# Top-k of the expert lookup: maxima beside the projections, lookups in bf16 between weight blocks

## The chip, the cores and the metric

One NeuronCore of a Trainium2 chip runs the whole program in one launch. The metric is device time in microseconds (us). The kernel before took 1478.95 us, the median of three runs (1477.77 to 1479.18).

## What is computed

The reference is a network of two blocks over 256 positions of width 1024, in float32. Only one part of it concerns the change: a layer of 16384 small experts (128 x 128 of them, reached by pairs of keys), with 8 heads.

```python
def peer_ffn(h, w_q, sub_keys, u, v):
    qh = (h @ w_q).reshape(t, PEER_HEADS, 2, PEER_HALF)
    s = jnp.einsum('thcd,hcnd->thcn', qh, sub_keys)
    s1, i1 = lax.top_k(s[:, :, 0], PEER_TOPK)          # 16 of 128, for each head
    s2, i2 = lax.top_k(s[:, :, 1], PEER_TOPK)
    cand = (s1[..., :, None] + s2[..., None, :])        # 256 sums
    cand_idx = (i1[..., :, None] * N_KEYS + i2[..., None, :])
    top_s, pos = lax.top_k(cand, PEER_TOPK)             # 16 of 256
    eidx = jnp.take_along_axis(cand_idx, pos, axis=-1)
    g = jax.nn.softmax(top_s, axis=-1)
    pre = jnp.einsum('cd,chkd->chk', hc, u[ec])
    coef = gc * jax.nn.gelu(pre, approximate=False)
    return jnp.einsum('chk,chkd->cd', coef, v[ec])
```

The kernel does not gather: it multiplies all experts' `u` with all positions, weighs the products by a routing matrix that holds the gates (zero where an expert was not chosen), and multiplies with all of `v`.

## The kernel before, in words

Weights come in blocks of 128 x 1024 float32 (512 KB). `weights` (L92) loads a block on SyncE's queue into one of four `wraw` buffers, rounds it on ScalarE to a high half `wh` (L98) and subtracts on an engine of choice to the low half `wl` (L100): "v" is VectorE, "g" is GpSimd. There are three buffers of `wh` and `wl`. A product block (`fm_block`, L133) is 24 products on TensorE, three for each of eight slices: high by high (L129), high by low (L130), low by high (L131), so the third product of a block is the first to need `wl`.

`peer` (L752) has these stages.

- The layer's input `hn` is made by `adaln` on VectorE and ScalarE (L278 to L281). 16 blocks of `peer_wq` give the queries `q`, one key set `j` each (head and half); the first two blocks are interleaved slice by slice. Low halves: blocks 0 and 1 on GpSimd, the others on VectorE. The sub-keys `sk` (1 MB) are loaded once (L767).
- `topk(tb)` for two blocks of 128 positions: the scores (L800, four key sets in one bank, copied by L801), then on VectorE the sixteen largest of each of 16 lists of 128 with their places (L803 to L807: eight largest, their places, replace, again), the 256 sums of each head (L810), sixteen of each of 8 lists of 256 (L815 to L819), and the lookup of the two key numbers by comparison, product and sum over 16 (L821 to L831), in float32.
- 128 blocks of `u` (`u_block`). The first 38, 43 and 46 (`N_PRE`) run while `topk` is going on, with their low halves on GpSimd; behind 38 come the exponentials (`exps`), behind 43 the gates (`gates`), transposed by TensorE (L849) into `rt`.
- 32 steps of `route`, eight positions each, make the routing matrix from five one-hot operations on VectorE (L882, L890) and 24 products (L895), and weigh what the u blocks left (L898); between them stand 2 and 3 u blocks in turn (`ROUTE_PER`), low halves on VectorE. Then the last u blocks, then 128 blocks of `v`.

The order on each engine is set at compile time by a planner, which takes the instructions by their place in the program among those that its own model holds ready, so that the instructions of two lists may be interleaved; on the chip each engine keeps that order. `issue_after` pins an instruction behind another of the same engine.

Of the kernel before, what the change touches and what calls it, by code (L numbers as in the profile page):

```python
# [9 lines left out]
FT = mybir.dt.float32  # L10
FR = mybir.dt.float32r
BF = mybir.dt.bfloat16
U32 = mybir.dt.uint32
AF = mybir.ActivationFunctionType
OP = mybir.AluOpType
# [9 lines left out]
TAKEN = -3.4e38  # L25
# [4 lines left out]
PLAN = "ijjaavaasvqvqvksskkssksqssrgrqsssrgss0gr1rggr0rrrgrg1rg20g31rg2rrg3rrgg23rg"  # L30
SPLIT = 4
FIRST = 2
N_PRE = (38, 43, 46)
ROUTE_PER = (2, 3)


class Scratch:
# [33 lines left out]
class Net:  # L71
# [104 lines left out]
    def sums(self, pool, cols=None):  # L176


        nc = self.nc
        n = 1 if cols is None else cols.shape[2]  # L180
        ps = self.ps([128, 2, n], "sm")
        behind = []

        def put():
            j, sq = behind.pop()
            rhs = self.ones[:, :1] if cols is None else cols[:, j]
            for tb in range(2):
                self.last_sum = nc.tensor.matmul(ps[:, tb], sq[:, tb * 128:tb * 128 + 128], rhs,  # L188
                                                 start=j == 0 and tb == 0, stop=j == KT - 1, skip_group_check=True)

        def take(x, j):
            if behind:
                put()
            sq = pool.tile([128, T], FT, name="sq", bufs=3)
            nc.scalar.activation(sq, x[:, j], AF.Square)
            behind.append((j, sq))

        def done():
            put()
            return ps  # L200
        return take, done
# [550 lines left out]
    def peer(self):  # L752
# [3 lines left out]
        with ExitStack() as es:  # L756
# [5 lines left out]
            def carve(name, *shape, dtype=FT):  # L762
                return tail.tile([128, *shape], dtype, name=name)
# [6 lines left out]
            for k in range(KT):  # L770
                o = slice(k * 128, k * 128 + 128)
                for ps, w in zip(pss, ws):
                    self.mm3(ps, (w[0][:, o], w[1][:, o]), (hn[0][:, k], hn[1][:, k]), k == 0, k == KT - 1)
            for j in range(16):
                ps = pss[j] if j < FIRST else self.fm_block(self.weights(ap["peer_wq"][j]), hn)
                nc.scalar.activation(q[:, j], ps, AF.Copy)
            io = self.io128
            rt = P.tile([128, 5, T], BF, name="rt")
            iob = P.tile([128, 128], BF, name="iob")
            nc.gpsimd.tensor_copy(iob, io)  # L780
            s_all = [carve(f"s{tb}", 16, 128) for tb in range(2)]
            cand = carve("cand", 8, 16, 16)
            prod = carve("prod", 128, 16)
            v16 = carve("v16", 16, 16)
            i16 = carve("i16", 16, 16, dtype=U32)
            i16f = carve("i16f", 8, 2, 16)
            top = carve("top", 8, 16)
            pos = carve("pos", 8, 16, dtype=U32)
            pc = carve("pc", 2, 128, dtype=U32)
            pf = i16.rearrange("p a b -> p (a b)").bitcast(FT).rearrange("p (c k) -> p c k", c=2)  # L790
            ies = [carve(f"ie{tb}", 3, 128) for tb in range(2)]

            def topk(tb):
                s = s_all[tb]
                ie = ies[tb]
                for g in range(4):
                    ps = self.ps([128, 4, 128], "acc")
                    for i in range(4):
                        j = 4 * g + i
                        nc.tensor.matmul(ps[:, i], q[:, j, tb * 128:tb * 128 + 128], sk[:, j], start=True, stop=True)  # L800
                    nc.scalar.activation(s[:, 4 * g:4 * g + 4], ps, AF.Copy)  # L801
                for j in range(16):
                    nc.vector.max(out=v16[:, j, :8], in_=s[:, j])  # L803
                    nc.vector.max_index(out=i16[:, j, :8], in_max=v16[:, j, :8], in_values=s[:, j])
                    nc.vector.match_replace(out=s[:, j], in_to_replace=v16[:, j, :8], in_values=s[:, j], imm_value=TAKEN)
                    nc.vector.max(out=v16[:, j, 8:], in_=s[:, j])
                    nc.vector.max_index(out=i16[:, j, 8:], in_max=v16[:, j, 8:], in_values=s[:, j])  # L807
                nc.vector.tensor_copy(i16f.rearrange("p h c k -> p (h c) k"), i16)
                v4 = v16.rearrange("p (h c) k -> p h c k", c=2)
                nc.vector.tensor_tensor(cand, v4[:, :, 0, :, None].to_broadcast([128, 8, 16, 16]),  # L810
                                        v4[:, :, 1, None, :].to_broadcast([128, 8, 16, 16]), op=OP.add)
                cf = cand.rearrange("p h a b -> p h (a b)")
                for h in range(8):
                    c = cf[:, h]
                    nc.vector.max(out=top[:, h, :8], in_=c)  # L815
                    nc.vector.max_index(out=pos[:, h, :8], in_max=top[:, h, :8], in_values=c)
                    nc.vector.match_replace(out=c, in_to_replace=top[:, h, :8], in_values=c, imm_value=TAKEN)
                    nc.vector.max(out=top[:, h, 8:], in_=c)
                    nc.vector.max_index(out=pos[:, h, 8:], in_max=top[:, h, 8:], in_values=c)  # L819
                posf = pos.rearrange("p h k -> p (h k)")  # L820
                nc.vector.tensor_scalar(pc[:, 0], posf, 4, None, op0=OP.logical_shift_right)  # L821
                nc.vector.tensor_scalar(pc[:, 1], posf, 15, None, op0=OP.bitwise_and)
                nc.vector.tensor_copy(pf, pc)
                eq = s.rearrange("p a (b c) -> p (a b) c", c=16)
                for c in range(2):
                    nc.vector.tensor_tensor(eq, io[:, None, :16].to_broadcast([128, 128, 16]),
                                            pf[:, c, :, None].to_broadcast([128, 128, 16]), op=OP.is_equal)
                    nc.vector.tensor_tensor(prod.rearrange("p (h k) j -> p h k j", h=8),
                                            eq.rearrange("p (h k) j -> p h k j", h=8),
                                            i16f[:, :, c, None, :].to_broadcast([128, 8, 16, 16]), op=OP.mult)  # L830
                    nc.vector.tensor_reduce(ie[:, c], prod, axis=AX.X, op=OP.add)  # L831
                g = ie[:, 2].rearrange("p (h k) -> p h k", h=8)
                nc.vector.tensor_tensor(g, top, top[:, :, 0:1].to_broadcast([128, 8, 16]), op=OP.subtract)

            def exps():
                with tc.issue_after(self.last_act.ins):
# [3 lines left out]
            def gates(tb):  # L840
                ie = ies[tb]
                g = ie[:, 2].rearrange("p (h k) -> p h k", h=8)
                st = P.tile([128, 8], FT, name="gst")
                nc.vector.tensor_reduce(st, g, axis=AX.X, op=OP.add)
                nc.vector.reciprocal(st, st)
                nc.vector.tensor_tensor(g, g, st[:, :, None].to_broadcast([128, 8, 16]), op=OP.mult)
                ps = self.ps([128, 3, 128], "sm")
                for c in range(3):
                    nc.tensor.transpose(ps[:, c], ie[:, c], self.ident)  # L849
                ts = slice(tb * 128, tb * 128 + 128)  # L850
                nc.vector.tensor_copy(rt[:, :2, ts], ps[:, :2])
                g = ps[:, 2]
                for z in range(3):
                    nc.vector.tensor_copy(rt[:, 2 + z, ts], g)
                    if z < 2:
                        nc.vector.tensor_tensor(ie[:, 0], g, rt[:, 2 + z, ts], op=OP.subtract)
                        g = ie[:, 0]

            def u_block(e, t, eng):

                ps = self.fm_block(self.weights(ap["peer_u"][e], eng), hn, out=self.ps([128, T], ("mm", "acc", "acc")[e % 3]))
                if t:
                    g = W.tile([128, T], FT, name="gelu", bufs=1)
                    self.last_act = nc.scalar.activation(g[:, :t], ps[:, :t], AF.Gelu)
                    nc.vector.tensor_mul(big[:, e, :t], big[:, e, :t], g[:, :t])
                if t < T:
                    self.last_act = nc.scalar.activation(big[:, e, t:], ps[:, t:], AF.Gelu)
# [30 lines left out]
                    nc.vector.tensor_mul(w[:, :n], pt[:, :n], w[:, :n])  # L898
                    nc.scalar.activation(w[:, n:], pt[:, n:], AF.Copy)

            topk(0)
            topk(1)
            e = 0
            for n, step in zip(N_PRE, (exps, lambda: [gates(tb) for tb in range(2)], lambda: 0)):
                while e < n:
                    u_block(e, 0, "g")
                    e += 1
                step()
            d = repeat(0)
# [608 lines left out]
```

## Time and profile before

| | |
|---|---|
| median of three runs | 1478.95 us |
| the profiled execution | 1477.79 us, span 1476.0 us |
| PE (TensorE) busy | 1389.3 us, 94% |
| DVE (VectorE) busy | 1103.3 us, 75% |
| ACT (ScalarE) busy | 755.4 us, 51% |
| POOL (GpSimd) busy | 247.5 us, 17% |
| mean granted TensorE clock | 0.982 |

Times in the rows are microseconds from the span's start, durations of a group's members nanoseconds. An arrow names what ended a wait. The busy time of PE overlaps itself, since products are pipelined: the number that a stretch started says more. The stage of this change lies from about 290 to 490 us: GpSimd has nearly all of its work between 355 and 482 us, DVE is full from 347 us on, PE is nearly full.

### The profile page before, as it was taken

The page shows a single profiled execution, that of the slowest core. Times are in us where ns is not written, and L with a number is a line of the kernel's source. Part 1 is how long each engine was busy: PE and PEld are TensorE (multiplying, and loading weights), DVE is VectorE, ACT ScalarE, POOL GpSimd, SP SyncE. Part 2 cuts the span into 40 slices and gives each one's busy share as a digit, 9 for nine tenths or more (in the row PEclk, how much of TensorE's full clock was granted, in tenths as well). Part 3 has the DMA queues.
Part 4 walks back from the last instruction along what each step waited for, and adds up shares of the span by engine and source line. Part 5 has one row for each costly group of instructions (what it writes and reads, how often), then busy time and mean ns, then how long its engine had stood idle before and what let it go on. Part 6 is the DMA issues. An engine that isn't in the chain of part 4 may idle for free. (4 is left out here: it accounts for less than half of the span.)

```text
span 1476.0 us, 28894 instructions
## 1 busy us (share of the span) xinstructions
PE 1389.3 (94%) x11584; PEld 1334.0 (90%) x11584; DVE 1103.3 (75%) x2044; ACT 755.4 (51%) x1358; POOL 247.5 (17%) x102
## 2 busy tenths in 40 slices
PE   4987988989998999999999999999999999899997
PEld 3876878989998999999999999999999889789996
DVE  7677868646999988999966555666557786777776
ACT  4544635445445555555454444444445465655555
POOL 3356532105999000000000000000000000000001
PEclk9999989999999999999999999999999999999998
DMA  7765854654555555555566665776564445256562
GB/s 281 250 199 201 280 175 161 205 193 156 174 184 166 173 154 168 158 159 157 165 194 216 202 190 190 228 233 215 186 187 157 128 134 171 72 173 196 189 191 95
DMA packets 76235, 269.52 MB, mean 183 GB/s; under 512 B 8970, under 2 KB 11202, under 8 KB 75460
## 3 DMA queue, kind: packets, MB, share of 16 engines
q1 hardware_dynamic: 71426, 257.99, 54.5%
q10 hardware_dynamic: 4674, 9.69, 1.9%
q8 instruction: 90, 1.47, 0.4%
q14 instruction: 45, 0.37, 0.1%
HBM read 265.01 MB, written 4.21 MB: 182 GB/s over the span
## 5 line engine op out<-in xcount | busy, mean ns | idle before, releaser
L98 ACT ACTIVATE wh<-wraw 128x1024 fp32r<-128x1024 f32 x431 | 456.2, 1060 | 521.1 <-PE ps_acc L130 243.1
L100 DVE TENSOR_TENSOR wl<-wraw,wh 128x1024 fp32r<-128x1024 f32 x346 | 423.9, 1227 | 245.3 <-ACT wh L98 243.9
L129 PE MATMUL ps_acc<-c,wh 128*128 128x256 f32 x1024 | 286.5, 280 | 0.0
L131 PE MATMUL ps_acc<-c,wl 128*128 128x256 f32 x1024 | 286.4, 280 | 0.0
L130 PE MATMUL ps_acc<-c,wh 128*128 128x256 f32 x1024 | 286.4, 280 | 0.0
L100 POOL TENSOR_TENSOR wl<-wraw,wh 128x1024 fp32r<-128x1024 f32 x85 | 228.1, 2700 | 194.0 <-ACT wh L98 151.2
L131 PE MATMUL ps_acc<-hn,wl 128*128 128x256 f32 x696 | 192.7, 277 | 6.2 <-POOL wl L100 6.2
L131 PE MATMUL ps_mm<-hn,wl 128*128 128x256 f32 x680 | 191.3, 282 | 6.4 <-POOL wl L100 6.4
L129 PE MATMUL ps_mm<-hn,wh 128*128 128x256 f32 x680 | 194.7, 286 | 2.0 <-ACT sga L446 1.0
L129 PE MATMUL ps_acc<-hn,wh 128*128 128x256 f32 x696 | 193.9, 279 | 0.0
L129 PEld LDWEIGHTS ps_acc<-c,wh 128*128 128x128 f32 x1024 | 192.5, 188 | 0.1
L130 PE MATMUL ps_acc<-hn,wh 128*128 128x256 f32 x696 | 192.4, 277 | 0.1
L130 PEld LDWEIGHTS ps_acc<-c,wh 128*128 128x128 f32 x1024 | 192.5, 188 | 0.0
L131 PEld LDWEIGHTS ps_acc<-c,wl 128*128 128x128 f32 x1024 | 192.5, 188 | 0.0
L130 PE MATMUL ps_mm<-hn,wh 128*128 128x256 f32 x680 | 191.5, 282 | 0.0
L1404 POOL TENSOR_TENSOR big<-big 128x512 f32<-128x512 f32 x4 | 5.0, 1264 | 982.0 <-DVE big L1401 982.0
L131 PEld LDWEIGHTS ps_mm<-hn,wl 128*128 128x128 f32 x680 | 130.8, 192 | 7.2 <-POOL wl L100 7.2
L131 PEld LDWEIGHTS ps_acc<-hn,wl 128*128 128x128 f32 x696 | 130.7, 188 | 7.2 <-POOL wl L100 7.2
L129 PEld LDWEIGHTS ps_mm<-hn,wh 128*128 128x128 f32 x680 | 131.3, 193 | 4.6 <-issue 1.3
L130 PEld LDWEIGHTS ps_mm<-hn,wh 128*128 128x128 f32 x680 | 131.0, 193 | 0.2
L130 PEld LDWEIGHTS ps_acc<-hn,wh 128*128 128x128 f32 x696 | 130.8, 188 | 0.3 <-DVE hn L281 0.3
L129 PEld LDWEIGHTS ps_acc<-hn,wh 128*128 128x128 f32 x696 | 130.6, 188 | 0.1
(484 smaller groups left out, 2821.9 us busy)
## 6 DMA issues: line engine op xcount, KB each, us to landing
wraw<-in_peer_u_dram SPq DMA_DIRECT2D x128, 512.0 KB, 3.9
wraw<-in_peer_v_dram SPq DMA_DIRECT2D x128, 512.0 KB, 4.2
wraw<-in_w_in_dram SPq DMA_DIRECT2D x70, 512.0 KB, 4.4
wraw<-in_ffn_up_dram SPq DMA_DIRECT2D x44, 512.0 KB, 3.6
wraw<-in_ffn_down_dram SPq DMA_DIRECT2D x22, 512.0 KB, 3.6
ada<-in_w_ada_dram SPq DMA_DIRECT2D x16, 512.0 KB, 6.5
wraw<-in_w_out_dram SPq DMA_DIRECT2D x16, 512.0 KB, 4.5
wraw<-in_peer_wq_dram SPq DMA_DIRECT2D x16, 512.0 KB, 3.6
```

The costliest lines, as they stand in the source:

```text
L98: nc.scalar.activation(h, raw, AF.Copy)
L100: (nc.vector if eng == "v" else nc.gpsimd).tensor_tensor(l, raw, h.bitcast(FT), op=OP.subtract)
L129: mm(out, a[0], b[0], start=first, stop=False, **kw)
L130: mm(out, a[0], b[1], start=False, stop=False, **kw)
L131: self.last_mm = mm(out, a[1], b[0], start=False, stop=last, **kw)
L1404: nc.gpsimd.tensor_tensor(xf[:, tb, cs], xt[:, tb, cs], fg[:, cs], op=OP.mult)
```

## The change

- The score products of a key set are issued in the loop over the key sets, behind the next set's projection, both blocks of positions in one bank; the scores are copied for each set, and its two lists' maxima follow there. The low halves of the `peer_wq` blocks in that loop go to GpSimd for three of four, to VectorE for the fourth (blocks 2, 4, 5, 6 to GpSimd, 3 and 7 to VectorE, and so on).
- Then come the sums of both blocks of positions, and the sixteen largest of all 16 lists of 256.
- The lookups compare, multiply and add in bf16 for both key numbers at once: 4096 elements an operation; the positions are first repeated four times by ScalarE (`pf4`). The sum over 16 is by halving adds. Each block of positions is done in four steps, one step ahead of each u block from block 18 to 25.
- GpSimd makes the low halves of the first 18 u blocks, VectorE those of all others. `exps` comes behind block 27, `gates` behind 29, the routing behind 31, with 3, 3, 3 and 2 u blocks between steps in turn, which leaves nine for the end instead of two.
- The candidates lie in `q`'s memory.

```diff
--- before.py
+++ after.py
@@ -30,8 +30,9 @@
 PLAN = "ijjaavaasvqvqvksskkssksqssrgrqsssrgss0gr1rggr0rrrgrg1rg20g31rg2rrg3rrgg23rg"
 SPLIT = 4
 FIRST = 2
-N_PRE = (38, 43, 46)
-ROUTE_PER = (2, 3)
+N_PRE = (27, 29, 31)
+ROUTE_PER = (3, 3, 3, 2)
+ONLY_MAXIMA = 18
 
 
 class Scratch:
@@ -771,66 +772,88 @@
                 o = slice(k * 128, k * 128 + 128)
                 for ps, w in zip(pss, ws):
                     self.mm3(ps, (w[0][:, o], w[1][:, o]), (hn[0][:, k], hn[1][:, k]), k == 0, k == KT - 1)
+            scores = carve("s", 32, 128).rearrange("p (t j) n -> p t j n", t=2)
+            v16 = carve("v16", 32, 16).rearrange("p (t j) k -> p t j k", t=2)
+            i16 = carve("i16", 32, 16, dtype=U32).rearrange("p (t j) k -> p t j k", t=2)
+
+            def sixteen(val, pos, of):
+
+                for half in (slice(0, 8), slice(8, 16)):
+                    nc.vector.max(out=val[:, half], in_=of)
+                    nc.vector.max_index(out=pos[:, half], in_max=val[:, half], in_values=of)
+                    if half.start == 0:
+                        nc.vector.match_replace(out=of, in_to_replace=val[:, half], in_values=of, imm_value=TAKEN)
+
+            def keys(j):
+
+                ps = self.ps([128, 2, 128], "sm")
+                for tb in range(2):
+                    nc.tensor.matmul(ps[:, tb], q[:, j, tb * 128:tb * 128 + 128], sk[:, j], start=True, stop=True)
+                nc.scalar.activation(scores[:, :, j], ps, AF.Copy)
+                for tb in range(2):
+                    sixteen(v16[:, tb, j], i16[:, tb, j], scores[:, tb, j])
+
             for j in range(16):
-                ps = pss[j] if j < FIRST else self.fm_block(self.weights(ap["peer_wq"][j]), hn)
+                ps = pss[j] if j < FIRST else self.fm_block(self.weights(ap["peer_wq"][j], "gggv"[j % 4]), hn)
                 nc.scalar.activation(q[:, j], ps, AF.Copy)
+                if j:
+                    keys(j - 1)
+            keys(15)
             io = self.io128
             rt = P.tile([128, 5, T], BF, name="rt")
             iob = P.tile([128, 128], BF, name="iob")
             nc.gpsimd.tensor_copy(iob, io)
-            s_all = [carve(f"s{tb}", 16, 128) for tb in range(2)]
...
+            cand = q.rearrange("p a (b c) -> p (a b c)", b=16).rearrange("p (t h x) -> p t h x", t=2, h=8)
+
+            def half(name, n):
+                return carve(name, n // 2).bitcast(BF)
+            i16f = half("i16f", 512).rearrange("p (t c h k) -> p t c h k", t=2, c=2, h=8)
+            top = carve("top", 2, 8, 16)
+            pos = carve("pos", 2, 8, 16, dtype=U32)
+            pc = carve("pc", 4, 128, dtype=U32).rearrange("p (t c) x -> p t c x", t=2)
+            pf = half("pf", 512).rearrange("p (t x) -> p t x", t=2)
+            pf4 = half("pf4", 1024).rearrange("p (x a) -> p x a", a=4)
             ies = [carve(f"ie{tb}", 3, 128) for tb in range(2)]
 
-            def topk(tb):
-                s = s_all[tb]
+            def sums():
+
+                for tb in range(2):
+                    v4 = v16[:, tb].rearrange("p (h c) k -> p h c k", c=2)
+                    nc.vector.tensor_tensor(cand[:, tb].rearrange("p h (a b) -> p h a b", a=16),
+                                            v4[:, :, 0, :, None].to_broadcast([128, 8, 16, 16]),
+                                            v4[:, :, 1, None, :].to_broadcast([128, 8, 16, 16]), op=OP.add)
+                    nc.vector.tensor_copy(i16f[:, tb].rearrange("p c h k -> p h c k"),
+                                          i16[:, tb].rearrange("p (h c) k -> p h c k", c=2))
+
+            def lookup(tb):
+
                 ie = ies[tb]
-                for g in range(4):
...
+                posf = pos[:, tb].rearrange("p h k -> p (h k)")
+                nc.vector.tensor_scalar(pc[:, tb, 0], posf, 4, None, op0=OP.logical_shift_right)
+                nc.vector.tensor_scalar(pc[:, tb, 1], posf, 15, None, op0=OP.bitwise_and)
+                nc.vector.tensor_copy(pf[:, tb], pc[:, tb].rearrange("p c x -> p (c x)"))
+                yield
+                nc.scalar.activation(pf4, pf[:, tb, :, None].to_broadcast([128, 256, 4]), AF.Copy)
+                eq, prod = (scores[:, i].rearrange("p a b -> p (a b)").bitcast(BF) for i in range(2))
+                shape = [128, 256, 4, 4]
+                nc.vector.tensor_tensor(eq.rearrange("p (x a b) -> p x a b", a=4, b=4),
+                                        iob[:, :16].rearrange("p (a b) -> p a b", a=4)[:, None].to_broadcast(shape),
+                                        pf4[:, :, None, :].to_broadcast(shape), op=OP.is_equal)
+                yield
+                shape = [128, 16, 16, 16]
+                nc.vector.tensor_tensor(prod.rearrange("p (h k j) -> p h k j", k=16, j=16),
+                                        eq.rearrange("p (h k j) -> p h k j", k=16, j=16),
+                                        i16f[:, tb].rearrange("p c h k -> p (c h) k")[:, :, None, :].to_broadcast(shape),
+                                        op=OP.mult)
+                yield
+                p3 = prod.rearrange("p (x j) -> p x j", j=16)
+                for n in (8, 4, 2):
+                    nc.vector.tensor_tensor(p3[:, :, :n], p3[:, :, :n], p3[:, :, n:2 * n], op=OP.add)
+                nc.vector.tensor_tensor(ie[:, :2].rearrange("p c x -> p (c x)"), p3[:, :, 0], p3[:, :, 1], op=OP.add)
                 g = ie[:, 2].rearrange("p (h k) -> p h k", h=8)
-                nc.vector.tensor_tensor(g, top, top[:, :, 0:1].to_broadcast([128, 8, 16]), op=OP.subtract)
+                t16 = top[:, tb]
+                nc.vector.tensor_tensor(g, t16, t16[:, :, 0:1].to_broadcast([128, 8, 16]), op=OP.subtract)
+                yield
 
             def exps():
                 with tc.issue_after(self.last_act.ins):
@@ -898,12 +921,17 @@
                     nc.vector.tensor_mul(w[:, :n], pt[:, :n], w[:, :n])
                     nc.scalar.activation(w[:, n:], pt[:, n:], AF.Copy)
 
-            topk(0)
-            topk(1)
+            sums()
+            for tb in range(2):
+                for h in range(8):
+                    sixteen(top[:, tb, h], pos[:, tb, h], cand[:, tb, h])
             e = 0
+            looks = [s for tb in range(2) for s in [lookup(tb)] * 4]
             for n, step in zip(N_PRE, (exps, lambda: [gates(tb) for tb in range(2)], lambda: 0)):
                 while e < n:
-                    u_block(e, 0, "g")
+                    if e >= ONLY_MAXIMA and looks:
+                        next(looks.pop(0))
+                    u_block(e, 0, "g" if e < ONLY_MAXIMA else "v")
                     e += 1
                 step()
             d = repeat(0)
```

## Rows read from the trace of the kernel before

**Rows 1.** The table by stretches: us, busy and starts per engine, granted clock, DMA.

```profile
300.00:310.00 10.00, 6.89 (x49) 6.67 (x48) 4.38 (x5) 4.55 (x8) 0.29 (x1) 0.87 0.62 203
366.00:376.00 10.00, 10.00 (x91) 10.00 (x90) 10.00 (x25) 4.90 (x8) 9.69 (x5) 1.00 0.57 168
...
396.00:406.00 10.00, 8.20 (x70) 7.81 (x69) 10.00 (x8) 4.28 (x7) 10.00 (x3) 1.00 0.51 159
406.00:416.00 10.00, 8.14 (x69) 7.95 (x70) 10.00 (x39) 3.20 (x6) 10.00 (x5) 1.00 0.50 148
...
456.00:466.00 10.00, 8.74 (x77) 8.55 (x76) 9.93 (x4) 7.08 (x10) 10.00 (x3) 1.00 0.46 132
466.00:476.00 10.00, 7.60 (x64) 7.21 (x63) 9.86 (x6) 3.99 (x6) 10.00 (x4) 1.00 0.41 138
476.00:486.00 10.00, 8.46 (x73) 8.22 (x72) 9.79 (x21) 3.11 (x6) 6.27 (x3) 1.00 0.69 209
...
600.00:700.00 100.00, 100.00 (x1023) 99.57 (x1022) 91.29 (x147) 51.41 (x127) 0.00 (x0) 1.00 0.51 159
```

The engines of that table stand in the order PE, PEld (PE's weight load), DVE, ACT, POOL.

**Rows 2.** Waits, 354 to 486 us: engine, line waited for: total, times, longest.

```profile
PE ps_acc L131 <- POOL wl L100: 4.7, 4, 1.4
...
PE ps_sm L849 <- DVE big L846: 1.5, 1, 1.5
```

**Rows 3.** Low halves on GpSimd: L100 (min/median/max ns), and a stretch of its timeline.

```profile
L100 POOL TENSOR_TENSOR wl<-wraw,wh x43: 2391/2412/4433, 355.8 to 479.8; 128x1024 fp32r<-128x1024 f32 x43
...
391.20 8.48 POOL L100 TENSOR_TENSOR wl<-wraw,wh 128x1024 fp32r<-128x1024 f32 x2 [0.31 <-ACT wh L98]
```

**Rows 4.** DVE's groups by line and form, 345 to 486 us: busy, mean ns.

```profile
L826 DVE TENSOR_TENSOR big<-io,big 128x2048 f32<-128x2048 f32 x4 | 17.7, 4423 | 0.0
```

**Rows 5.** DVE operations of two inputs: one row of the timeline, one of L882.

```profile
256.57 0.42 DVE L119 TENSOR_TENSOR mg<-m,mg 128x256 fp32r<-128x256 f32 x1
...
L882 DVE TENSOR_TENSOR oa<-iob,rt x32: 679/680/692, 483.5 to 729.9; 128x1024 bf16<-128x1024 bf16 x32
```

**Rows 6.** DVE's groups by line, 486 to 745 us (the routing).

```profile
L100 DVE TENSOR_TENSOR wl<-wraw,wh 128x1024 fp32r<-128x1024 f32 x80 | 97.7, 1221 | 25.4 <-ACT wh L98 25.1
...
L865 DVE TENSOR_TENSOR big<-big,gelu 128x16 f32<-128x16 f32 (+30 forms) x77 | 21.9, 284 | 0.0
```

**Rows 7.** Score products: L800 (min/median/max ns), and four of them in PE's timeline.

```profile
L800 PE MATMUL ps_acc<-big x64: 270/275/552, 307.8 to 351.7; 128*128 128x128 f32 x64
L800 PEldq EVENT_SEMAPHORE  x4: 51/51/4988, 302.4 to 307.7; - x4
...
308.78 1.05 PE L800 MATMUL ps_acc<-big 128*128 128x128 f32 x4
```

**Rows 8.** DVE's timeline: first maxima of successive pairs of lists, 128 and 256 wide.

```profile
349.65 0.47 DVE L803 MAX8 big<-big 128x8 f32<-128x128 f32 x2
...
351.98 0.47 DVE L803 MAX8 big<-big 128x8 f32<-128x128 f32 x2
...
374.57 0.73 DVE L815 MAX8 big<-big 128x8 f32<-128x256 f32 x2
...
378.24 0.73 DVE L815 MAX8 big<-big 128x8 f32<-128x256 f32 x2
```

**Rows 9.** ScalarE's timeline: a high half in the u phase.

```profile
395.50 1.06 ACT L98 ACTIVATE wh<-wraw 128x1024 fp32r<-128x1024 f32 x1 [1.39 <-POOL wl L100]
```

**Rows 10.** DVE's timeline while `hn` is made.

```profile
294.02 2.69 DVE L281 SCALAR_TENSOR_TENSOR hn<-hn,mod,hn 128x256 fp32r<-128x256 f32 x2 [0.24 <-ACT hn L280]
...
297.31 1.21 DVE L100 TENSOR_TENSOR wl<-wraw,wh 128x1024 fp32r<-128x1024 f32 x1
298.44 0.87 DVE L281 SCALAR_TENSOR_TENSOR hn<-hn,mod,hn 128x256 fp32r<-128x256 f32 x2
```

**Rows 11.** DVE's groups by line and form again, 345 to 486 us: small operations.

```profile
L808 DVE CAST big<-big 128x256 f32<-128x256 uint32 x2 | 5.0, 2487 | 0.0
...
L833 DVE TENSOR_TENSOR big<-big 128x128 f32<-128x128 f32 x2 | 0.5, 270 | 0.0
```

More of the change, by code (lines that the diff above doesn't have):

```diff
@@ L780, in peer @@
             nc.gpsimd.tensor_copy(iob, io)
-            s_all = [carve(f"s{tb}", 16, 128) for tb in range(2)]
[L782 to L790, printed above, removed]
@@ L791, in peer @@
-            ies = [carve(f"ie{tb}", 3, 128) for tb in range(2)]
-            def topk(tb):
-                s = s_all[tb]
-                ie = ies[tb]
-                for g in range(4):
[L797 to L831, printed above, removed]
```

## The prediction

> **What bounds the kernel now.** I read the totals first: TensorE (PE) is busy nearly all the span, so only its holes can be won back. Then the table by stretches. At full pace PE starts 90 to 91 products in 10 us; five stretches of the u phase that changes start fewer: 70, 69, 77, 64 and 73 [rows 1]. They are short of 90.5 by 20.5, 21.5, 13.5, 26.5 and 17.5, in all 99.5 products; at 10/90.5 = 0.11 us each that is 11.0 us. The other stretches from 320 to 486 us start 90 or 91, and the routing behind them, with its smaller products, has PE busy throughout, so 11.0 us is what this change can win.
>
> Then the waits of that phase: PE waits for `wl` (the low half of a weight block) from GpSimd, and once for a gate that VectorE (DVE) makes [rows 2]. Why is GpSimd late? A low half takes it 2.41 us in the median and 4.43 at the longest; PE takes 2.72 us a block (each `wl` begins 2.72 after the last: 2.41 and an idle 0.31). In one row it needs 8.48 us for two, where 2.72 + 2.41 = 5.13 would be on time [rows 3]. Just then DVE has its long lookups: 2048-element operations of two inputs, 4.42 us each [rows 4]. A 256-element one took 0.42 and the 1024-element low half 1.22 [rows 5, 6], so 1.04 ns an element and 0.15 fixed, which makes 2.29 for 2048. The other 2 us of the 4.42, and the lateness of GpSimd, are each engine waiting until the other's instruction has ended. Being 3.35 late (8.48 - 5.13) cost PE a wait of 1.4 [rows 2], so GpSimd runs about 1.9 us ahead of PE's need.
>
> **The change part by part.**
>
> *Scores and maxima in the key loop.* The products are the same 64 records, now four behind each of 16 key sets [rows 7]: 28 records, 3.1 us of PE per set, where before it was 24 per set and the rest at the end. No gain or loss for PE. DVE's maxima of two lists together take 351.98 - 349.65 = 2.33 us [rows 8], and a set has just two lists. With one low half in four (1.22/4) DVE needs 2.6 us per set, under 3.1; GpSimd has three lows in four, 1.8 per set. So 37 us of DVE work goes under PE's projections, and I cost it at nothing. The cover fails if the two lists of a set are not interleaved: one list alone is some 1.6 us, a set 3.2, and DVE, at 3.5 us a set against PE's 3.1, ends some 7 us late. In DVE's queue every fourth set's low half stands among maxima that wait for ScalarE's score copy; if one stood behind maxima not yet ready, PE would wait for both. ScalarE's 16 smaller copies for 8 are hidden: its high half, 1.06 us in 2.72 [rows 9], leaves room. The weight loads keep their order on SP's queue.
>
> *Start of the loop.* Block 2's low half moves from DVE to GpSimd, at about 296 us, while DVE still makes the normalised input `hn`. The row of block 1 shows the price: two L281 operations took 2.69 with GpSimd's low beside them, 0.87 later without [rows 10]: 1.8 lost, at most a whole 2.4. DVE gives up its own 1.21. Between -0.9 (the low leaves the chain, nothing blocks) and +2.4, I take +1.2. The sub-keys' load is issued after the last `hn` and PE's queue then stands 4.99 us at the first score product [rows 7]; the wait is put down to a high half, which these products don't read, so I take it for the load. Hence this delay is not absorbed. The Trainium skill, "SBUF — State Buffer", section "SBUF: two separate sides", says that the pair of ports which VectorE and GpSimd share goes to one of them for a whole instruction, and the other stands still. The trace agrees (2.69 against 0.87). By the rule this item is a loss of 1.2; if the two engines only shared a rate it would be near -0.9 and the total 2 us better.
>
> *All sums first.* Two 2048-element sums and two casts, with GpSimd's lows beside them: up to 4.4 and 2.5 each [rows 4, 11], some 13 us of DVE. GpSimd is held for twice 2.29, recovers 0.31 in each of three blocks, and has 1.9 ahead: 4.6 - 0.9 - 1.9 = 1.8 for PE. Between 0 and 2.7, I take 1.5. Then 16 lists of 256: a pair takes 378.24 - 374.57 = 3.67 [rows 8], 29.4 us, which block no one (one input: GpSimd stayed at 2.41 beside them). The last key set, sums and lists: 2.3 + 13 + 29.4 = 45 us, beside 18 blocks of 2.72 = 49. Hidden.
>
> *Lookups in bf16, between blocks 18 to 25, whose lows are on DVE.* The nearest row for a bf16 operation of two inputs is the one-hot of 1024, 0.68 us, with the same pattern of four innermost elements [rows 5]: less 0.15 that is 0.52 ns an element. So 4096 elements cost 2.3. The four steps of one block of queries: integer operations and a cast, 0.6 (bounds 0.5 and, with the cast of the old rows, 3); comparison 2.3; product 2.3; adds of 2048, 1024, 512 and 256 and the difference, 1.2 + 0.7 + 0.4 + 0.4 + 0.3 = 3.0. That is 8.2, twice 16.4, and eight lows 9.8: 26.2 us against 8 x 2.72 = 21.8. Less the lead of about 2: 2.4. Starts overlap by some 0.1, so I take 2.0; from 0 up to 14.6, where all goes at float32's 1.04 ns: 4.4 + 4.4 + 4.9 + 0.6 = 14.3, twice 28.6, + 9.8 - 21.8 - 2. I stay near the low end, since the row of the same form decides. ScalarE's copy of 1024 before each comparison (1.06, as rows 9) can hold DVE if it stands behind a high half that waits for PE; a low half lies between.
>
> *Gates and routing.* L846 no longer meets GpSimd (128 elements: 0.27 at L833, rows 11), PE's wait of 1.5 there shrinks; I keep 0.8 (0 to 1.8). Routing has 2.75 blocks a step in place of 2.5: a step of 8.1 us (486 to 745, 32 steps) holds 7.4 of DVE, its share from 600 to 700 [rows 1]; a quarter block more is 0.67 of PE and 0.25 x (1.22 + 0.28) = 0.38 of DVE [rows 6], so 7.8 in 8.8: PE still binds, DVE at 89% instead of 91%. Nothing gained or lost; the same 128 blocks, nine instead of two behind the routing.
>
> *Sum.* -11.0 + 1.2 + 1.5 + 2.0 + 0.8 = -5.5 us. The profiled execution took 1477.79, span 1476.0 and 1.8 around it: 1472.3. The median of the runs shown is 1.16 higher: **1473.5**.
>
> **Rivals.**
> - *DVE becomes the bound (slower).* From block 0 to the first routing step DVE has 45 + 16.4 + 13 lows 15.9 + gates 5 (some 20 operations like L833's) + the first five one-hots 3 = 85 us, PE 31 x 2.72 = 84. There is no reserve and GpSimd no longer helps, so every us more on DVE is one on PE. At the float32 rate: -11.0 + 1.2 + 1.5 + 14.6 + 0.8 = +7.1, 1486. Lists not paired (7 us late) give 1480. It decides from 5.5 us of extra DVE work on. For: the balance; the adds' short rows of 8, 4 and 2. Against: the one-hots' 0.68, the pairs in [rows 8]. 0.15.
> - *The front takes the gain (about even).* PE's order is written by a planner; if it puts the first key set's score products into the middle of block 2, PE waits there for the sub-keys' load (4.99 us now, [rows 7]) with up to a block, 2.7 us, behind it, and block 3's high half behind that on ScalarE. TensorE's granted clock is 0.87 in the stretch of that wait [rows 1], part of it at 1.2 instead of 2.4 GHz: four score records behind the wait take 1.05 us [rows 7], near twice the 0.11 each. With 1.2 for the start and 1 to 2 us more at the lower level this is 5 to 6: -11.0 + 1.5 + 2.0 + 0.8 + 5.5 = -1.2, 1476 to 1479. For: the score products have become more urgent than block 2. Against: the load may well be late in the plan too. 0.2.
> - *All hidden.* The maxima give DVE enough lead, no lock meets PE's need: -11.0 + 1 = 1469. For: the lead of 1.9. Against: 85 against 84 us. 0.13.
> - The forecast, 1470.5 to 1476.5: 0.47. The last 0.05 is for what I have not seen, either side.
>
> **How the numbers follow.** About 0.2% (3 us) is what a measurement of this kernel can tell from no change. Faster by more: 0.40 of the forecast, all of the hidden case, and a little of the front's and the unseen: 0.57. Same: 0.07 of the forecast, most of the front, a bit of the DVE case: 0.24. Slower: most of the DVE case, a tail of the front: 0.19. The range 1467.5 to 1481 leaves out the float32 rate and the best of the hidden case; the likeliest case's own range is 1470.5 to 1476.5.
>
> **What would show it.** Right: key-set maxima on DVE between 309 and 357 us and PE at 90 products per 10 us there; from 357 one short loss at the sums, GpSimd's 4 us lows only there; the comparison of 4096 near 2.3 us; small waits of PE for `wl` from DVE at blocks 20 to 26; none for GpSimd behind block 18; routing at full pace. Wrong: a comparison or product of 4 us, MAX8 of single lists, PE waiting at the first score products longer than 3.1, or DVE's lows late from block 18 on by more than 4 us in all.

## The result, and the profile after

The changed kernel took 1489.83 us in the median (1485.91 to 1491.3, five runs) beside 1479.18 for the kernel before (1477.77 to 1480.18, five): ratio 1.0072, 95% interval 1.0057 to 1.0087. It is slower; 1473.5 was forecast, and 1481 was the upper end of the range.

The profiled execution took 1489.44 us (1477.79 before): +11.65. The stage that changes, from the first `hn` product of `peer_wq` to the first product of the `v` blocks, takes 474.00 us in place of 463.38: +10.62. What lies ahead of it took 1.74 longer and what follows 0.70 less. So the loss is inside the stage.

The table by stretches of the changed kernel, as [rows 1]: us, busy time and starts of PE, PEld, DVE, ACT, POOL, then the granted clock and the DMA share.

```profile
340.00:350.00 10.00, 10.00 (x89) 10.00 (x88) 8.69 (x50) 5.04 (x10) 4.80 (x2) 1.00 0.53 159
366.00:376.00 10.00, 9.05 (x80) 8.85 (x79) 10.00 (x24) 3.99 (x6) 10.00 (x5) 1.00 0.60 181
380.00:390.00 10.00, 10.00 (x91) 10.00 (x90) 10.00 (x44) 4.42 (x8) 9.16 (x5) 1.00 0.69 209
390.00:400.00 10.00, 5.45 (x49) 5.25 (x47) 10.00 (x47) 0.00 (x0) 0.80 (x1) 0.89 0.26 90
400.00:410.00 10.00, 4.06 (x17) 3.77 (x18) 9.48 (x13) 5.77 (x8) 6.64 (x2) 0.50 0.18 52
410.00:420.00 10.00, 7.56 (x59) 7.36 (x58) 9.90 (x6) 3.99 (x6) 4.42 (x2) 0.93 0.34 107
420.00:430.00 10.00, 7.91 (x57) 7.91 (x58) 8.54 (x9) 2.43 (x4) 0.00 (x0) 0.83 0.58 162
430.00:440.00 10.00, 10.00 (x91) 10.00 (x90) 4.90 (x4) 4.44 (x8) 0.00 (x0) 1.00 0.66 204
456.00:466.00 10.00, 9.49 (x95) 9.21 (x94) 10.00 (x20) 4.72 (x10) 0.00 (x0) 1.00 0.56 182
```

The holes of [rows 1] at 456 to 486 are gone, and the key loop runs at 89 products. In their place one pit stands between 390 and 430 us: 49, 17, 59 and 57 products. Two columns of the row from 390 matter most: ScalarE, busy for 4.42 of 10 us in the row before, did nothing at all in 10 us, and VectorE was busy throughout. From 400 on the granted clock is 0.50, the lower of its two levels (1.2 GHz).

Waits of the changed kernel, 354 to 486 us (line waited for, total, times, longest), as [rows 2]; in this kernel L99 makes the high half, L101 the low half, L834 casts the positions, L836 is ScalarE's copy `pf4`, L839 is the comparison, L844 the product, L851 and L852 the adds, and L130 to L132 are the three products of TensorE.

```profile
POOL wl L101 <- ACT wh L99: 16.0, 8, 12.4
...
ACT big L836 <- DVE big L834: 12.5, 1, 12.5
...
PE ps_mm L130 <- ACT wh L99: 7.7, 1, 7.7
ACT wh L99 <- DVE wl L101: 7.6, 1, 7.6
...
PE ps_mm L132 <- DVE wl L101: 4.5, 1, 4.5
...
PE ps_mm L132 <- POOL wl L101: 3.7, 2, 2.8
```

The second of these lines is new and heads the chain. ScalarE's own timeline (start, duration, line, operation; in brackets the idle time before and what ended it) shows where the copy stands:

```profile
387.26 1.06 ACT L99 ACTIVATE wh<-wraw 128x1024 fp32r<-128x1024 f32 x1 [1.39 <-issue]
388.22 0.36 ACT L890 ACTIVATE big<-ps_acc 128x256 f32<-128x256 f32 x1
401.10 1.06 ACT L836 ACTIVATE big<-big 128x1024 bf16<-128x1024 bf16 x1 [12.51 <-DVE big L834]
402.06 1.04 ACT L99 ACTIVATE wh<-wraw 128x1024 fp32r<-128x1024 f32 x1
403.01 0.37 ACT L890 ACTIVATE big<-ps_mm 128x256 f32<-128x256 f32 x1
404.51 1.06 ACT L836 ACTIVATE big<-big 128x1024 bf16<-128x1024 bf16 x1 [1.14 <-DVE big L839]
```

In the program the first copy comes ahead of u block 19. The planner put it behind the gelu of block 11 (the row at 388.22, L890): presumably its model held the cast ready there; no run shows the model itself. On the chip VectorE was still in the 16 lists of 256, and the cast came at 400.77. Each engine keeps its order, so block 15's high half, due at 390 in the rhythm of 2.72 us, stood behind the copy and started at 402.06. PE used up blocks 12 to 14 and stopped:

```profile
395.17 0.28 PE L132 MATMUL ps_acc<-hn,wl 128*128 128x256 f32 x1
403.15 0.58 PE L130 MATMUL ps_mm<-hn,wh 128*128 128x256 f32 x1 [7.71 <-ACT wh L99]
403.53 0.41 PE L131 MATMUL ps_mm<-hn,wh 128*128 128x256 f32 x1
406.74 0.58 PE L132 MATMUL ps_mm<-hn,wl 128*128 128x256 f32 x1 [2.79 <-POOL wl L101]
```

Then the same lateness shows on GpSimd (its 12.4 in the waits), whose low halves of blocks 15 to 17 now fall beside the lookups. VectorE's timeline:

```profile
400.77 0.29 DVE L834 CAST big<-big 128x256 bf16<-128x256 uint32 x1
...
402.19 2.29 DVE L839 TENSOR_TENSOR big<-iob,big 128x4096 bf16<-128x4096 bf16 x1 [0.45 <-ACT big L836]
404.51 4.32 DVE L844 TENSOR_TENSOR big<-big 128x4096 bf16<-128x4096 bf16 x1
408.87 3.28 DVE L851 TENSOR_TENSOR big<-big 128x2048 bf16<-128x2048 bf16 x1
412.07 4.49 DVE L839 TENSOR_TENSOR big<-iob,big 128x4096 bf16<-128x4096 bf16 x1
...
418.61 2.29 DVE L844 TENSOR_TENSOR big<-big 128x4096 bf16<-128x4096 bf16 x1
420.82 2.35 DVE L101 TENSOR_TENSOR wl<-wraw,wh 128x1024 fp32r<-128x1024 f32 x2
```

Two things are to be seen. Alone, an operation of 4096 takes 2.29 us, the price forecast; beside GpSimd 4.3 to 4.5. And the first low half on VectorE, that of block 18, comes only at 420.82, behind both comparisons and both products: the planner set the lookups ahead of the low halves, and not between them. PE stopped for it from 417.28 to 422.09.

Adding up the stage (a hole is the time beyond 0.11 us between two starts that lie over 0.3 apart; the clock's part is the time beyond 0.11 us of the closer starts that fall where the granted clock is 0.50: 8 of them before, 32 after) gives most of the loss; the pinned kernel is the first experiment below:

| us | before | after | pinned |
|---|---|---|---|
| holes at the start of the loop and the first scores | 5.98 | 5.28 | 5.44 |
| GpSimd's late low halves, sums, gates, first routing step | 10.01 | 1.80 | 1.63 |
| blocks 15 to 18 | 0 | 16.47 | 0 |
| products at the lower clock | 0.82 | 3.32 | 0 |
| length of the stage | 463.38 | 474.00 | 455.13 |

After less before by these rows: -0.70 - 8.21 + 16.47 + 2.50 = +10.06, measured +10.62. Pinned less before: -0.54 - 8.38 - 0.82 = -9.74, measured -8.25. The rows leave out 0.56 and 1.49, small differences over some 4200 other starts; the largest single one, about 1.1 and 1.2, lies in the key loop (see the terms below).

### The profile page after: what moved, and what is told of

It is laid out like the page before. It is cut to its first block, busy times and chain, and to the rows that moved or that the text cites. A ratio compares the mean times of both kernels' runs of the same rounds, so it can differ in the third digit from the quotient of the medians.

```text
span 1487.7 us, 28951 instructions
## 1 busy us (share of the span) xinstructions
PE 1398.6 (94%) x11584; PEld 1342.5 (90%) x11584; DVE 1095.3 (74%) x2077; ACT 759.5 (51%) x1377; POOL 193.5 (13%) x84
## 5 line engine op out<-in xcount | busy, mean ns | idle before, releaser
L99 ACT ACTIVATE wh<-wraw 128x1024 fp32r<-128x1024 f32 x431 | 456.1, 1060 | 518.2 <-PE ps_acc L131 269.9
L101 DVE TENSOR_TENSOR wl<-wraw,wh 128x1024 fp32r<-128x1024 f32 x364 | 446.3, 1228 | 258.2 <-ACT wh L99 256.8
L130 PE MATMUL ps_acc<-c,wh 128*128 128x256 f32 x1024 | 286.6, 280 | 0.0
L132 PE MATMUL ps_acc<-c,wl 128*128 128x256 f32 x1024 | 286.5, 280 | 0.0
L130 PE MATMUL ps_mm<-hn,wh 128*128 128x256 f32 x680 | 198.7, 292 | 8.9 <-ACT wh L99 8.3
L132 PE MATMUL ps_mm<-hn,wl 128*128 128x256 f32 x680 | 195.4, 287 | 12.3 <-POOL wl L101 7.7
L101 POOL TENSOR_TENSOR wl<-wraw,wh 128x1024 fp32r<-128x1024 f32 x67 | 174.2, 2611 | 180.4 <-ACT wh L99 129.6
L131 PE MATMUL ps_mm<-hn,wh 128*128 128x256 f32 x680 | 194.7, 286 | 0.0
L130 PE MATMUL ps_acc<-hn,wh 128*128 128x256 f32 x696 | 194.2, 279 | 0.0
L132 PE MATMUL ps_acc<-hn,wl 128*128 128x256 f32 x696 | 192.4, 277 | 1.5 <-POOL wl L101 1.5
L130 PEld LDWEIGHTS ps_acc<-c,wh 128*128 128x128 f32 x1024 | 192.5, 188 | 0.1
L132 PEld LDWEIGHTS ps_acc<-c,wl 128*128 128x128 f32 x1024 | 192.5, 188 | 0.0
L132 PEld LDWEIGHTS ps_mm<-hn,wl 128*128 128x128 f32 x680 | 134.1, 197 | 13.4 <-POOL wl L101 8.6
L130 PEld LDWEIGHTS ps_mm<-hn,wh 128*128 128x128 f32 x680 | 134.4, 198 | 11.4 <-ACT wh L99 8.7
L131 PEld LDWEIGHTS ps_mm<-hn,wh 128*128 128x128 f32 x680 | 134.3, 198 | 0.1
L132 PEld LDWEIGHTS ps_acc<-hn,wl 128*128 128x128 f32 x696 | 130.6, 188 | 1.7 <-POOL wl L101 1.7
L130 PEld LDWEIGHTS ps_acc<-hn,wh 128*128 128x128 f32 x696 | 130.7, 188 | 0.2 <-ACT hn L281 0.2
```

Of the source, the lines that this page charges most:

```text
L99: nc.scalar.activation(h, raw, AF.Copy)
L101: (nc.vector if eng == "v" else nc.gpsimd).tensor_tensor(l, raw, h.bitcast(FT), op=OP.subtract)
L130: mm(out, a[0], b[0], start=first, stop=False, **kw)
L131: mm(out, a[0], b[1], start=False, stop=False, **kw)
L132: self.last_mm = mm(out, a[1], b[0], start=False, stop=last, **kw)
```

## The experiments

The theory after the first look: ScalarE's queue, held by the copy, and the order that the early copy gives VectorE, make the whole loss. The rivals: VectorE has too little time in any order (the prediction's "DVE becomes the bound"), or the key loop costs what the lookups win (near its "The front takes the gain"). Eight kernels were run, 6 to 12 executions each, with ratios to the kernel before on the same chip; its medians there were 1478.22 (first four) and 1480.44 us (last four).

**The copy held where the program has it.** `last_act` is the latest gelu in program order.

```diff
-                nc.scalar.activation(pf4, pf[:, tb, :, None]..., AF.Copy)
+                with tc.issue_after(self.last_act.ins):
+                    nc.scalar.activation(pf4, pf[:, tb, :, None]..., AF.Copy)
```

> The changed kernel, with ScalarE's copy of the positions pinned behind the gelu of the u block that stands before it in the program (blocks 18 and 22), nothing else. Theory A, the copy's place in ScalarE's queue: the planner put both copies behind block 11's gelu, where the first waited 12.5 us for VectorE's cast with the high halves behind it. Without that the PE holes of 8.0, 3.2 and 4.8 us and the products at the lower clock go: about 1474, 1472 to 1477, and no wait of ScalarE on the cast over 2 us. Rival B, VectorE has more work than TensorE from block 0 on: the holes turn into waits for VectorE's low halves, 1485 or more.

1470.85 us (1468.0 to 1474.01), ratio 0.9947 (0.9925 to 0.9968): 19 us less than the changed kernel, faster than the kernel before, and 1.2 us below the range written for it. The same stretches, columns as above:

```profile
390.00:400.00 10.00, 10.00 (x91) 10.00 (x90) 10.00 (x42) 5.32 (x8) 5.64 (x3) 1.00 0.57 194
400.00:410.00 10.00, 10.00 (x90) 10.00 (x90) 7.87 (x7) 5.95 (x9) 0.00 (x0) 1.00 0.61 210
410.00:420.00 10.00, 10.00 (x90) 10.00 (x89) 9.93 (x9) 5.39 (x10) 0.00 (x0) 1.00 0.59 181
420.00:430.00 10.00, 10.00 (x91) 10.00 (x90) 9.93 (x10) 7.18 (x11) 0.00 (x0) 1.00 0.58 182
```

The pit is gone and the clock stays at 1.00. ScalarE's copy (L837 here) waits for nothing, and VectorE's low halves lie between the steps (L840 is the comparison, L845 the product):

```profile
404.77 1.05 ACT L837 ACTIVATE big<-big 128x1024 bf16<-128x1024 bf16 x1
```

```profile
398.94 2.35 DVE L101 TENSOR_TENSOR wl<-wraw,wh 128x1024 fp32r<-128x1024 f32 x2
401.97 1.23 DVE L101 TENSOR_TENSOR wl<-wraw,wh 128x1024 fp32r<-128x1024 f32 x1 [0.68 <-ACT wh L99]
404.64 1.23 DVE L101 TENSOR_TENSOR wl<-wraw,wh 128x1024 fp32r<-128x1024 f32 x1 [1.45 <-ACT wh L99]
405.86 2.29 DVE L840 TENSOR_TENSOR big<-iob,big 128x4096 bf16<-128x4096 bf16 x1
408.06 1.22 DVE L101 TENSOR_TENSOR wl<-wraw,wh 128x1024 fp32r<-128x1024 f32 x1
409.20 2.29 DVE L845 TENSOR_TENSOR big<-big 128x4096 bf16<-128x4096 bf16 x1
```

One pinned instruction thus repaired both queues: with the copy late in the plan, the comparison behind it is late too. Two more kernels separate them.

**The copy on VectorE**: ScalarE's queue has no such wait any more, VectorE's order stays the planner's.

```diff
-                nc.scalar.activation(pf4, pf[:, tb, :, None]..., AF.Copy)
+                nc.vector.tensor_copy(pf4, pf[:, tb, :, None]...)
```

> The changed kernel with the copy of the positions made by VectorE instead of ScalarE, so that ScalarE's queue waits for nothing of the lookup; the planner still sets most of both lookups ahead of block 18's low half on VectorE. If the hold of ScalarE's queue alone made the loss (A, narrow): about 1475. If the planner's early place of the lookups also counts (A, wide): the low half of block 18 is ready some 12 us after the last maxima (400 us), about 8 us late, and the next ones follow more lookup work: 1484 to 1489, with TensorE waiting for low halves of VectorE and not for high halves. Rival B says 1488 or more, with the waits spread over blocks 18 to 31.

1481.01 us (1477.67 to 1484.88), ratio 1.0016 (0.9997 to 1.0036). One hole is left, 9.97 us long; waits and the rows of VectorE on either side of it:

```profile
PE ps_mm L132 <- DVE wl L101: 9.8, 1, 9.8
```

```profile
396.85 0.69 DVE L836 COPY big<-big 128x1024 bf16<-128x1024 bf16 x1
...
407.59 0.62 DVE L852 TENSOR_TENSOR big<-big 128x256 f32<-128x256 bf16 x1
408.12 1.22 DVE L101 TENSOR_TENSOR wl<-wraw,wh 128x1024 fp32r<-128x1024 f32 x1
```

Block 18's low half, which PE needs at 399.4, stands behind 11 us of lookups. So VectorE's order alone costs some 10 us against the pinned kernel; up to 1.4 of the 11 is the two copies themselves, 0.69 each, which VectorE now makes too. The narrow reading, about 1475, falls; the time lies 3 us under what was written for the wide one, near the kernel before.

**ScalarE held, VectorE's order kept.** The first copy stands behind block 12's gelu; every lookup step is pinned behind the latest low half on VectorE, so that the low halves lie between the steps.

```diff
+                with tc.issue_after((self.last_act if tb else self.acts[12]).ins):
                     nc.scalar.activation(pf4, pf[:, tb, :, None]..., AF.Copy)
...
-                        next(looks.pop(0))
+                        with tc.issue_after(self.last_v.ins):
+                            next(looks.pop(0))
```

> The changed kernel with VectorE's order kept as in the pinned kernel (low halves between the lookup steps), but with ScalarE's first copy of the positions placed behind the gelu of block 12, where it was behind block 11's in the changed kernel and behind block 18's in the pinned one. Theory (the copy holds ScalarE's queue, and the high halves behind it are late): the copy waits about 9.5 us for VectorE's cast, one block (2.7) less than the 12.5 of the changed kernel, TensorE's holes at 397 to 407 us are one block shorter than the 11.2 there, about 8.5; time 1470.9 + 8.5 = 1479, from 1476.5 to 1481.5. Rival (only VectorE's order matters, the held copy is covered by the high halves made ahead): no hole over 1 us, 1469 to 1473.

1479.84 us (1474.28 to 1490.06), ratio 1.0 (0.9978 to 1.0021). The waits, 380 to 480 us, ScalarE's row, and two of VectorE's that show a low half behind the comparison (in this kernel L132 is the first product of a block, L836 the cast, L839 the copy, L842 the comparison):

```profile
ACT big L839 <- DVE big L836: 9.7, 1, 9.7
...
PE ps_acc L132 <- ACT wh L99: 4.9, 1, 4.9
```

```profile
397.25 1.06 ACT L839 ACTIVATE big<-big 128x1024 bf16<-128x1024 bf16 x1 [9.71 <-DVE big L836]
...
405.03 2.28 DVE L842 TENSOR_TENSOR big<-iob,big 128x4096 bf16<-128x4096 bf16 x1
407.76 1.23 DVE L101 TENSOR_TENSOR wl<-wraw,wh 128x1024 fp32r<-128x1024 f32 x1 [0.46 <-ACT wh L99]
```

The copy waited 9.7 us as expected, and PE's holes there are 5.07, 0.27, 1.95 and 0.27, in all 7.56 where 8.5 was expected; the rival's "no hole over 1 us" falls. The stage takes 465.36, 10.2 over the pinned one: 7.6 of holes, 0.5 at the sums, and 2.7 of products at the lower clock (26 of them, none in the pinned kernel; granted 0.62 from 400 to 410 us), which my sum had left out, less 0.7 at the start, the gates and the routing. So either cause alone takes the whole gain. In the changed kernel the hold makes 11.5 of the holes (7.87, 0.27, 3.09, 0.27). The other 5.0 (4.70 and 0.27) stand at block 18's low half, behind the lookups in VectorE's order; but the two causes are not cleanly apart there, since three operations of the lookups (4.32, 3.28 and 4.49) took 6.3 us longer beside GpSimd's low halves, which the hold had made late.

**More time for VectorE**: low halves of the first 24 blocks on GpSimd, lookups from block 24.

```diff
-N_PRE = (27, 29, 31)
-ONLY_MAXIMA = 18
+N_PRE = (33, 35, 37)
+ONLY_MAXIMA = 24
```

> The changed kernel with the lookups six blocks later in the program (low halves of the first 24 u blocks on GpSimd, exponentials, gates and routing behind 33, 35 and 37): 16 us more time for VectorE. The planner's order has ScalarE's copies still behind block 11's gelu. Theory A: the hole of 8 us at the copy stays where it is, about 395 us; the lows on GpSimd meet the lookups and cost some more; 1484 to 1491. Rival B: VectorE now has time enough, the holes go, 1474 to 1478.

1489.08 us (1485.55 to 1490.96), ratio 1.0068 (1.0044 to 1.0092), no better than the changed kernel. Its waits:

```profile
ACT big L836 <- DVE big L834: 12.5, 1, 12.5
...
PEld ps_mm L130 <- ACT wh L99: 7.9, 1, 7.9
```

The copy does not move, though the program asks for it six blocks later, and the hole of 7.85 is the same: VectorE's shortage of time is not the cause of it. (PE's wait for VectorE's low half shrank from 4.5 to 0.3; later collisions with GpSimd came instead, holes of 1.12 and 1.54. This run alone can't tell whether that part was time or order; the pinned kernel can, which has no more time and no such wait.)

**The key loop alone**: the kernel before with the scores and maxima of the key sets in the loop and the loop's low halves as in the changed kernel; lookups in float32 as before.

```diff
-                ps = ... self.fm_block(self.weights(ap["peer_wq"][j]), hn)
+                ps = ... self.fm_block(self.weights(ap["peer_wq"][j], "gggv"[j % 4]), hn)
                 nc.scalar.activation(q[:, j], ps, AF.Copy)
+                if j:
+                    keys(j - 1)
+            keys(15)
```

> The kernel before with one part of the change alone: score products and maxima of each key set in the projection loop, with that loop's division of the low halves; sums, lists and float32 lookups as before, block after block of positions, the first 46 low halves of u on GpSimd. A and B both hold the loop for nearly free (0.6 us at its start); the collisions of GpSimd with the long lookups stay, earlier by 37 us: 1478 to 1481. Rival C, the loss comes from the loop (VectorE late, TensorE's order): 1484 or more.

1480.68 us (1475.62 to 1485.26), ratio 1.0013 (0.9992 to 1.0034). The loop neither costs nor gives anything that the time shows: the float32 lookups still collide with GpSimd (six holes of 1.0 to 1.55 between 394 and 448 us, one of 1.57 at the sums). The pinned kernel's gain therefore lies in the rest of the change, the lookups and the low halves that go to VectorE with them; no run takes those two apart.

**Terms of the sum, on the pinned kernel.** Block 2's low half back on VectorE; the casts of the key numbers moved from the sums into the first lookup step; both.

```diff
-                ps = ... self.weights(ap["peer_wq"][j], "gggv"[j % 4]) ...
+                ps = ... self.weights(ap["peer_wq"][j], "v" if j == 2 else "gggv"[j % 4]) ...
```

> The pinned kernel with the low half of peer_wq block 2 on VectorE again. By the prediction's term for the start of the loop (+1.2): TensorE's holes between 292 and 312 us, 5.4 in the pinned kernel, shrink by about 1.2, time 1469.7. Rival (block 2's low half on GpSimd costs nothing, since the holes there are those of the score products and of hn): holes 5 to 6 as in the kernel before, time 1470 to 1472.

1470.54 us (1466.48 to 1474.78), ratio 0.9925 (0.9898 to 0.9952). The holes at the start shrink from 5.44 to 4.89, not by 1.2 and just out of the rival's 5 to 6: those at `hn` go back to 0.28, but PE's stop at the first score product grows from 1.97 to 2.67, and the granted clock falls to 0.50 behind it, so that PE reaches the u blocks no earlier (58.2 us from the first `hn` product, 57.8 in the pinned kernel). The time cannot be told from the pinned kernel's.

```diff
             def sums():
-                    nc.vector.tensor_copy(i16f[:, tb]..., i16[:, tb]...)
...
             def lookup(tb):
                 nc.vector.tensor_copy(pf[:, tb], pc[:, tb]...)
+                nc.vector.tensor_copy(i16f[:, tb]..., i16[:, tb]...)
```

> The pinned kernel with the two casts of the key numbers moved from the sums (beside GpSimd's low halves, 2.4 to 2.5 us each there) into the first step of the lookups. Theory (the hole at the sums is GpSimd being held by VectorE's long operations): the casts take 0.3 us each without GpSimd's low halves beside them, the hole of 0.6 us at 367 goes, the maxima end 4 us earlier; time 1470.2, from 1468.5 to 1471.5. Rival (the hole comes from the two sums alone): the hole stays at 0.6, time 1470.9.

1473.57 us (1470.43 to 1475.84), ratio 0.9949 (0.9923 to 0.9975): not better, and both expectations of the hole were wrong. Both sums now follow each other, so that two long low halves of GpSimd do too (4.09 and 4.42 us; in the pinned kernel one of 2.46 lies between 3.99 and 4.46), and the hole is 1.42 (0.60 in the pinned kernel, 1.11 in that of block 2, both with the casts between the sums):

```profile
357.20 7.67 DVE L822 TENSOR_TENSOR big<-big 128x2048 f32<-128x2048 f32 x2
```

```profile
PE ps_acc L132 <- POOL wl L101: 1.3, 1, 1.3
```

So the sums make the hole; the casts between them, for all that they take 2.5 us beside GpSimd, add nothing to it.

> Both of the last two edits together: by the sum of their terms 1.2 + 0.6 under the pinned kernel, 1469; if neither term is real, 1470.9. It is the candidate for the fastest version, 0.993 of the kernel before.

1472.75 us (1469.52 to 1481.43), ratio 0.9947 (0.9929 to 0.9966), no gain over the pinned kernel: neither term is worth anything that can be measured. (PE's stop at the first score products is 4.49 in this profile, 1.97 in the pinned one.)

## Why the prediction was wrong

**The step that failed** is the lookups: "bf16, between blocks 18 to 25, whose lows are on DVE", 2.0 us, with bounds 0 and 14.6. It took the program's order for the order on the engines. The description of the kernel says that a planner takes instructions by its own model of what is ready; I used that for the score products of the first key set, a rival, and not for the lookups. Two results of it were missing:

- ScalarE's copy. I weighed that it "can hold DVE if it stands behind a high half", and not the reverse: an instruction that waits for VectorE holds the high halves queued behind it on ScalarE. That is the rule by which I judged VectorE's fourth-set low halves, and it was not applied to the added instruction on ScalarE. The wait was 12.5 us against the 7.0 of products that PE still had in hand (388.2 to 395.2).
- VectorE's order: lookups ahead of the low halves of blocks 18 and on.

The trace shows the queue's rule in one pair of rows: the copy idle for 12.51 us and the high half right behind it. The Trainium skill, "PSUM — Partial Sum Buffer", section "Engine vs sequencer instructions", calls the queues of ScalarE, VectorE and GpSimd "strict FIFO", which agrees; read beside the added copy it would have raised the question.

Measured for the step: 16.47 of holes in place of 2.0, above even the 14.6 at the float32 rate, and 3.3 at the lower clock, which no term of the sum held. With the copy where the program has it (pinned) the step cost no hole at all. Two of the signs that I had set down for "wrong" came: an operation of 4096 over 4 us (4.32, 4.49), though from GpSimd beside it and not from its own rate, and a low half of VectorE late by more than 4 us (4.70).

**The other terms.**

- Holes removed: 11.0 forecast, 10.0 by PE's starts, and none of the removed ones came back.
- Key loop: nearly right. 3.2 us a set, two lists interleaved, VectorE in time. But PE made 88 to 89 products in 10 us and not 90, since in every set one product next to the scores starts 0.20 us after the one before, in place of 0.11: about 0.1 us a set, some 1.1 to 1.2 in all against the kernel before, where the term had nothing.
- Start of the loop: +1.2 forecast, -0.7 measured (-0.54 pinned). The price at `hn` was there: the holes of the hn products grow from 0.28 to 1.85 (1.11, 0.41, 0.33). But it was absorbed, which I had excluded: PE's stop at the first score product fell from 3.28 to 1.76, and three small ones of 0.24 to 0.25 went. (The 4.99 of [rows 7] is the wait in PE's queue; the engine itself stood for 3.28.)
- Sums: 1.5 forecast, 1.12 measured, 0.60 pinned. Single rows answer to [rows 4, 11]:

```profile
358.55 3.27 DVE L822 TENSOR_TENSOR big<-big 128x2048 f32<-128x2048 f32 x1
361.74 2.49 DVE L825 CAST big<-big 128x256 bf16<-128x256 uint32 x1
364.14 4.49 DVE L822 TENSOR_TENSOR big<-big 128x2048 f32<-128x2048 f32 x1
368.56 2.46 DVE L825 CAST big<-big 128x256 bf16<-128x256 uint32 x1
```

- Comparison and product 2.3 each: 2.29. The adds in the pinned kernel: 1.22, 0.72, 0.69 and 0.65 for 1.2, 0.7, 0.4 and 0.4: the last two, with rows of two and one, cost as much as 512 and 480 elements at float32's 1.04 ns, 0.5 us a block of queries more than forecast.
- Gates and routing: 0.8 forecast, 0.68 measured (1.03 pinned); the routing keeps its pace.

**The rivals.** The right sign came from "DVE becomes the bound", but not for its reason: it wanted 5.5 us of extra work on VectorE; the operations' own times were near the forecast, and six blocks more time for them left the total where it was (1489.08). The balance of 85 against 84 us which stood for it was no obstacle either: in the pinned kernel VectorE is busy 9.93 of 10 us in both stretches from 410 to 430 and PE does not wait for it there. The front did not take the gain. The pinned kernel, which is the change as I had read it, took 1470.85: 1.9 from "All hidden" (1469), 2.7 from the forecast of 1473.5 and within its range. That is partly luck, since terms that were too dear (lookups, start of the loop, sums) made up for 1.0 too much in removed holes and for the key loop.

The Trainium skill, "SBUF — State Buffer", section "SBUF: two separate sides", gives the ports that VectorE and GpSimd share to one of them for a whole instruction. The traces here agree for bf16 too: 2.29 us alone, 4.32 and 4.49 with GpSimd's low halves beside, and a low half of 3.51 in place of 2.40. It is a second effect in the pit and not its origin, since GpSimd's blocks 15 to 17 were only there because ScalarE had held them back.

## What to carry to other kernels

Where a compiler orders the engines' queues by a model, the program's order is a wish: for each added instruction that waits on another engine, ask where its queue will have it and what stands behind it, and weigh the wait against the work that the next engine has in hand. Here an added operation of 1 us on a queue that was busy for 4.42 of 10 us in the stretch before made holes of 11.5 us. A pin behind an instruction that is certainly late is cheap insurance: 0.9947 in place of 1.0072 here.

## What the runs showed that I had not expected

After PE's stop of 8 us the granted clock was 0.50 for the next stretch and products started 0.21 us apart in place of 0.11; in the changed kernel this added 3.3 us to 16.5 of holes, in the one with ScalarE held 2.7 to 7.6, and in the one with the copy on VectorE 1.9 to 10.2. In the pinned kernel the granted clock stayed at 1.00 through the whole stage. A hole cost more than its length.
